# Late rows of a feed-forward, taken between later down projections instead of in the first two groups

## The chip, the cores and the metric

The kernel runs on one core of one Trainium2 chip. The metric is the time of one execution in microseconds of the device, smaller is better. The engines are TensorE (PE in the profile, its weight loads PEld), VectorE (DVE), ScalarE (ACT), GpSimd (POOL) and SyncE (SP), which issues nearly all DMAs in one queue that is worked in order. Each engine, too, takes its instructions in a fixed order.

## The reference

One layer of an encoder on 2048 rows of 1024 numbers (float32). An RMS norm, a combined projection, two kinds of attention and an output projection come first; what matters here is what follows:

```python
h = h + jnp.einsum('bse,ed->bsd', mix, w_out[l])      # output projection, residual

u2 = rms_norm(h, norm2_w[l])
gate = jnp.einsum('bsd,df->bsf', u2, w_gate[l])       # D_FF = 2816
up = jnp.einsum('bsd,df->bsf', u2, w_up[l])
h = h + jnp.einsum('bsf,fd->bsd', jax.nn.silu(gate) * up, w_down[l])
```

## The kernel before

Every matrix product is made of float16 parts: an operand is split into a high and a low half, and three products (high by high, high by low, low by high) are added up. In the feed-forward each 2 x 2 block product is formed with seven products instead of eight (Strassen's way, as Winograd arranged it), so a weight has seven combinations, each with two halves (`[P, 7, 2, 512]`), and so has an operand X.

The feed-forward works in two halves of 1024 rows, and in each half in 11 groups of 256 of the 2816 inner columns: 22 steps, half 0 first. The groups are counted from zero in the code (`fg`) and in the loop (`i`); the third group is `fg` 2. One step does `gate` (84 matrix instructions in seven products, L1030), then `up` (84 more), which multiplies the two and writes the product's combinations into an `act` tile (two buffers). After every second group comes a `down`, with two act tiles and two `wd` tiles (168 instructions, L1138): it stands at the third, fifth, seventh group and so on, between that step's gate and up. `down` takes the residual rows from DRAM (`hd`) into tiles `hs` (four buffers of 128 x 1024 float32, two in a pair), adds to them (L1144), and stores them back (L1187).

While a step computes, the weights of the next one are prepared. `load_ffn` is a generator: it fetches a weight into one of two `stages` buffers (L923, L925), squares it on ScalarE into the only `sq` buffer (L190 or L954), has TensorE find the column sums (`fsc`, L963, or L183 for a down weight), derives a scale by small VectorE operations, and writes the halves: the high ones on ScalarE (L216) or GpSimd (L220), the low ones on VectorE (L221), the combinations' sums on GpSimd (L98). The finished weight is also stored to DRAM (`split`, L919), and half 1 loads it from there (L944). Gate and up weights share two buffers (`wgu`), down weights have two of their own (`wd`). Where the generators advance is written out by hand: `quad`, which does the seven products of a gate or an up, calls a hook after each product (`at(1)` to `at(7)`), and `in_gate` and `in_up` move the generators from there. In a `quad` the second sum of products into `pd` has to wait for the evacuation of the first one (L1057 on VectorE).

The operands X are the normalised rows of `h`, transposed, combined and split. For rows 0 to 1535 that is done in the output projection (`post`). The last four tiles of 128 rows (12 to 15, the row pairs `j` = 2 and 3 of half 1) are left for later, since half 1 needs them only at step 11: these are the **late rows**. `build_x` does them, as a generator with `yield` between its pieces: load of the gain and of two row tiles (L1191, L1203), norms (`norm_tile`: a square on ScalarE, L226, the power on GpSimd, L156, the scaling on VectorE, L229), 16 transposes on TensorE (L1213, behind the last matrix instruction written so far) with ScalarE copying back (L1214), and `x_ops`: four combinations (L98) and four pieces of splitting, the high half on ScalarE (L89), the low one on VectorE or GpSimd (L98), each stored to `xcd` (L238). It takes all four `hs` buffers (as `bx`) for the gain, two row tiles and scratch, and one of the two `wd` buffers (as `b16`) to store from. The line `late_at` says after which products of which steps it moves on: those of the first two groups. Hooks 1 to 7 are those of the gate, 8 to 14 those of the up.

The order of the instructions on each engine is made by a scheduler of the programming framework from the order of the program, in which the earlier instruction has the higher priority, and from its own model of when each can start. So what stands earlier in the program usually, but not always, comes first on an engine. Which engine splits what is picked by running sums of estimated cost (`pick`, `to16`, `tt`).

Of the kernel before, what the change touches and what calls it, by code (L numbers as in the profile page):

```python
# [11 lines left out]
F32 = mybir.dt.float32  # L12
F16 = mybir.dt.float16
# [3 lines left out]
ALU = mybir.AluOpType  # L17
# [4 lines left out]
S, D, P = 2048, 1024, 128  # L22
# [37 lines left out]
def block(tc, a, out):  # L60
    nc = tc.nc
    PE, ACT, DVE, POOL, SP = nc.tensor, nc.scalar, nc.vector, nc.gpsimd, nc.sync
    top = ExitStack()
    with top:
# [44 lines left out]
        def nm(s):  # L109
            uid[0] += 1  # L110
            return f"{s}{uid[0]}"
# [57 lines left out]
        hd = dr.tile([NT, P, D], F32, name="hd")  # L169
# [87 lines left out]
        with ExitStack() as ph1:  # L257
# [24 lines left out]
            r_1, p_1, _ = norm_gain(None, w1[:, :D])  # L282
# [591 lines left out]
        with ExitStack() as ph2:  # L874
# [9 lines left out]
            fd = ph2.enter_context(tc.tile_pool(name="fd", bufs=2, reuse_waits="tile"))  # L884
# [8 lines left out]
            r_2, p_2, r_24 = rp2  # L893
            scales = {}

            rows = []
            front = [None]

            def behind():
# [5 lines left out]
            def stage(fg, nme):  # L905
                st = stages[:, turn[0]]
                turn[0] ^= 1
                f0 = 256 * fg
                with tc.issue_after(rows[1].ins) if (fg, nme) == (1, "u") else nullcontext():
                    fetch(st, f0, nme)  # L910
                store(0)
                return st

# [7 lines left out]
            def fetch(st, f0, nme):  # L921
                if nme == "d":
                    SP.dma_start(st.rearrange("p (f n) -> p f n", f=2), a["w_down"][0, f0 : f0 + 256, :].rearrange("(f p) n -> p f n", p=P))  # L923
                else:
                    SP.dma_start(st.rearrange("p (k n) -> p k n", k=KT), a["w_gate" if nme == "g" else "w_up"][0, :, f0 : f0 + 256].rearrange("(k p) n -> p k n", p=P))  # L925
# [149 lines left out]
            def gate(W, X, hooks):  # L1075
# [11 lines left out]
                note("A", 2000)  # L1087
                return sg

            def up(W, X, sg, hooks, final=False):  # L1090
                if final:
                    act = stages[:].rearrange("p b n -> p (b n)").bitcast(F16)[:, :7168].rearrange("p (o s n) -> p o s n", o=7, s=2)
                else:
                    act = fp.tile([P, 7, 2, 512], F16, tag="act", bufs=2, name=nm("act"))

                def put(o, src):
                    ACT.copy(act[:, o, 0], src)  # L1097
                    note("A", 500)
                    tt(act[:, o, 1], src, act[:, o, 0], ALU.subtract, 512, LE)

                def on_up(f, t, c):
                    s = sg[f, t][:]
                    DVE.scalar_tensor_tensor(s, c[:], W["F"][:], s, op0=ALU.mult, op1=ALU.mult)  # L1103
                    if (f, t) != (0, 1):
                        put({(0, 0): 0, (1, 0): 1, (1, 1): 3}[f, t], s)
                        return
                    a11, a12, a21, a22 = (sg[k][:] for k in ((0, 0), (1, 0), (0, 1), (1, 1)))
                    s3 = fp.tile([P, 512], F32, tag="cu", bufs=CU, name=nm("cu"))
                    tt(s3[:], a11, a21, ALU.subtract, 512, SE)
                    tt(a21, a21, a22, ALU.add, 512, SE)  # L1110
                    put(2, a21)
                    tt(a11, a21, a11, ALU.subtract, 512, SE)
                    tt(a12, a12, a11, ALU.subtract, 512, SE)
                    put(6, a12)
                    put(4, a11)
                    put(5, s3[:])

                quad(W["u"], X, "cu", CU, on_up, hooks)
                note("D", 2440)
                return act  # L1120
# [66 lines left out]
                        SP.dma_start(out[t * P : (t + 1) * P, :] if last else hd[t], hs[j][q][:])  # L1187

            def build_x():
                w2f, xa, xb, xt = (hp.tile([P, D], F32, tag="hs", bufs=4, name=nm("bx")) for _ in range(4))  # L1190
                SP.dma_start(w2f[:], a["norm2_w"].partition_broadcast(P))  # L1191
                DVE.tensor_scalar(w2f[:], w2f[:], r_24[:], None, op0=ALU.mult)
                b16 = fd.tile([P, 7, 2, 512], F16, tag="wd", bufs=2, name=nm("b16"))[:].rearrange("p o s n -> p (o s n)")
                n = [0]

                def bufs():
                    n[0] = (n[0] + 1) % 3
                    return b16[:, 2048 * n[0] : 2048 * n[0] + 2048]

                d2 = lambda z: z[:].rearrange("p (d n) -> p d n", d=2)  # L1200
                for j in (2, 3):
                    for q, z in enumerate((xa, xb)):
                        rows.append(SP.dma_start(z[:], hd[8 + 2 * j + q]))  # L1203
                    yield
                    for z in (xa, xb):
                        norm_tile(z[:], z[:], w2f[:], xt[:])
                    yield
                    for z in (xa, xb):
                        for h in range(2):
                            tr = pst("xtr")  # L1210
                            with behind():
                                for k in range(4):
                                    PE.transpose(tr[:, P * k : P * k + P], z[:, 512 * h + P * k : 512 * h + P * k + P], id32[:])  # L1213
                            ACT.copy(z[:, 512 * h : 512 * h + 512], tr[:])  # L1214
                        note("A", 1000)
                    yield
                    yield from x_ops([d2(z) for z in (xa, xb)], d2(xt), 1, j, bufs, "AP", "DP")

            W = {}
            X = [None] * 7  # L1220
# [20 lines left out]
            fp = ph2.enter_context(tc.tile_pool(name="fp", bufs=2, reuse_waits="tile"))  # L1241
# [3 lines left out]
            def tick(n):  # L1245
                for _ in range(n):
                    next(ticks, None)

            tick(1)
            load_now(0, 0, "d", W)  # L1250

            steps = [(h, f) for h in range(2) for f in range(NFG)]
            units = []
            hs = None
            chains = {}
            late_at = ((5, 9, 10, 11, 12, 13, 14), (3, 7, 8, 9, 10, 11, 12))
            for i, (half, fg) in enumerate(steps):
                if i == NFG:
                    load_x(1, XL)
                due = (len(units) == 2 and i + 1 < len(steps)) or (fg == 0 and units)  # L1260
                if due:
                    dh = steps[i - 1][0]
                    hs = [load_hs(dh, 0)]
                Wn = {}
                more = i + 1 < len(steps)

                def go(key, n=1):
                    for _ in range(n):
                        next(chains.get(key, iter(())), None)

                def start(key, *args):
                    chains[key] = load_ffn(*args)
                    go(key)

                def row(s):
                    if i < 2 and s in late_at[i]:
                        tick(1)

                def in_gate(s):
                    if s == 1:  # L1280
                        if more:
                            start("g", *steps[i + 1], "g", Wn)
                    elif s < 5:
                        go("u")
                    elif s == 5:
                        go("u", 9)
                        if more and i > 0:
                            start("d", half, fg, "d", W)
                    else:
                        go("g")  # L1290
                    row(s)

                def in_up(s):
                    if s < 3:
                        go("g")
                    elif s == 3:
                        go("g", 9)
                        go("d")
                        if more:
                            start("u", *steps[i + 1], "u", Wn)  # L1300
                    elif s < 6:
                        go("d")
                    elif s == 6:
                        go("d", 9)
                    else:
                        go("u")
                    row(7 + s)

                sg = gate(W, X, in_gate)
                if not more:  # L1310
                    load_now(half, fg, "d", W)
                if due:
                    down(dh, units, hs, dh != half, lambda: go("g"))
                    units = []
                act = up(W, X, sg, in_up, not more)
                if more and steps[i + 1][0] == 1:
                    go("u", 9)
                units.append((W, act))
                if not more:
                    down(half, units, [load_hs(half, 0, True)], True)  # L1320
                W = Wn
# [24 lines left out]
```

## Time and profile before

| | us |
|---|---|
| median of 3 runs | 2681.76 (2677.7 to 2685.48) |
| the profiled execution | 2682.59 |
| its span (first to last instruction) | 2680.8 |
| start of the feed-forward's gate in it | 1427.2 |
| mean granted TensorE clock | 0.984 of full speed |

The busy times of the engines come with their share of the span. In a row of a wait stand the engine, what it did then, the engine that ended the wait with its line, and the total, the count and the longest in us. In a row of the timeline stand the start and length in us, the engine, the line, the operation, the tiles (out<-in) with the shape, the count, and in brackets the idle time before it and what ended that. In a row of a tile's or line's instructions stand the least, median and greatest duration in ns. A busy TensorE is not TensorE at its peak, and its ends are modelled.

### The profile page before, as it was taken

To read this page: it belongs to the slowest core of one execution; us is meant where nothing else is said; L and a number is where in the kernel's file an instruction comes from. 1 tells how busy PE (TensorE), PEld (TensorE's weight loads), DVE (VectorE), ACT (ScalarE), POOL (GpSimd) and SP (SyncE) were. 2 spreads that over 40 slices of the span, in tenths; PEclk is the share of its full clock that TensorE was granted. 3 is DMA by queue.
4 is the path that set the end of the run, shared out by engine and by line. 5 is a ranking of instruction groups with operands and counts; after the bars stand their busy time and mean duration, and the time that the engine had idled before them with its cause. 6 is when DMAs were issued, how large, how long until landed. Compare 5 with 4: busy or idle time off the path is not lost. (4 is left out here: it accounts for less than half of the span.)

```text
span 2680.8 us, 50579 instructions
## 1 busy us (share of the span) xinstructions
PE 2492.4 (93%) x19628; PEld 1498.6 (56%) x19628; DVE 1932.7 (72%) x3711; ACT 1347.0 (50%) x2487; POOL 1489.1 (56%) x1098
## 2 busy tenths in 40 slices
PE   6998989888988989889989899999999999999999
PEld 4655656577776776557775344444444444444444
DVE  6898969898989989877766868777685544444434
ACT  4665656567978878665644535344352112111121
POOL 2578667667767766546764656565564232322323
PEclk9999999999999999999999899999999999999999
DMA  6777697767998979987897574665649743635532
GB/s 222 213 162 181 146 200 168 179 143 184 193 179 179 185 160 209 210 191 217 218 285 282 208 250 178 255 226 202 245 183 346 293 177 143 233 141 186 195 111 95
DMA packets 619585, 534.41 MB, mean 199 GB/s; under 512 B 480640, under 2 KB 548224, under 8 KB 609104
## 3 DMA queue, kind: packets, MB, share of 16 engines
q1 hardware_dynamic: 617520, 529.09, 69.9%
q8 instruction: 154, 2.52, 0.4%
q0 software_dynamic: 512, 1.36, 0.2%
q14 instruction: 87, 0.71, 0.1%
q10 hardware_dynamic: 1312, 0.72, 0.1%
HBM read 261.08 MB, written 147.32 MB: 152 GB/s over the span
## 5 line engine op out<-in xcount | busy, mean ns | idle before, releaser
L98 POOL TENSOR_TENSOR s<-z,s 128x1024 f16<-128x1024 f32 (+7 forms) x288 | 472.0, 1647 | 142.5 <-ACT s L89 109.8
L507 PE MATMUL sc<-kT,qT 128*128 128x512 f16 (+3 forms) x1520 | 382.0, 353 | 53.3 <-DVE z L623 19.3
L622 DVE TENSOR_TENSOR_SCAN z<-z,sc 128x512 f32<-128x512 f32 (+3 forms) x320 | 352.8, 1112 | 58.6 <-ACT sc L620 38.0
L1138 PE MATMUL pd<-wd,act 128*128 128x512 f16 x1764 | 390.9, 379 | 1.2 <-DVE cg L1071 1.2
L326 PE MATMUL pj<-w,xt 128*128 128x384 f16 x1920 | 352.2, 331 | 18.8 <-ACT xt L683 6.9
L1030 PEld LDWEIGHTS <-wg 128*128 128x128 f16 x1848 | 182.0, 99 | 230.2 <-issue 16.4
L518 PE MATMUL yp<-v,aT 128*128 128x64 f16 (+1 forms) x4896 | 269.8, 204 | 41.6 <-DMA aT<-s 40.2
L518 PEld LDWEIGHTS <-aT 128*128 128x128 f16 x4896 | 237.5, 99 | 120.4 <-DMA aT<-s 52.5
L1030 PEld LDWEIGHTS <-wu 128*128 128x128 f16 x1848 | 180.7, 98 | 218.0 <-issue 2.6
L98 POOL TENSOR_TENSOR act<-cg,act 128x512 f16<-128x512 f32 x112 | 148.5, 1337 | 262.9 <-ACT act L1097 150.8
L1138 PEld LDWEIGHTS <-act 128*128 128x128 f16 x1764 | 172.8, 98 | 209.4 <-issue 2.8
L326 PEld LDWEIGHTS <-xt 128*128 128x128 f16 x1920 | 187.3, 99 | 147.5 <-issue 21.4
L89 ACT CAST s<-z 128x128 f16<-128x128 f32 (+7 forms) x215 | 173.1, 809 | 134.1 <-DMA aT<-s 40.5
L98 POOL TENSOR_TENSOR hs<-hs,cu 128x512 f32<-128x512 f32 x99 | 130.9, 1328 | 171.3 <-DVE hs L1144 70.8
L619 ACT ACTIVATE z<-sc,c 128x512 f32<-128x512 f32 (+3 forms) x320 | 210.7, 663 | 25.6 <-PE sc L507 11.7
L1097 ACT CAST act<-cg 128x512 f16<-128x512 f32 x126 | 77.3, 616 | 238.4 <-DVE cg L1103 162.7
L507 PEld LDWEIGHTS <-qT 128*128 128x128 f16 x1520 | 128.4, 99 | 121.0 <-DVE z L623 23.0
L832 PE MATMUL po<-wo,mt 128*128 128x256 f16 x1536 | 180.7, 277 | 13.9 <-DVE xf L835 8.4
L1030 PE MATMUL pm<-X,wu 128*128 128x512 f16 x792 | 180.4, 379 | 1.3 <-DVE wu L221 1.3
L1030 PE MATMUL pm<-X,wg 128*128 128x512 f16 x792 | 181.3, 382 | 0.0
L342 PE MATMUL pj<-xt,w 128*128 128x128 f16 x2304 | 175.0, 220 | 6.7 <-DVE v L364 5.7
L1144 DVE SCALAR_TENSOR_TENSOR hs<-pd,c,hs 128x512 f32<-128x512 f32 x136 | 99.0, 747 | 109.6 <-PE pd L1138 83.1
(266 smaller groups left out, 4737.6 us busy)
## 6 DMA issues: line engine op xcount, KB each, us to landing
xt<-xs SPq DMA_DIRECT2D x112, 512.0 KB, 4.3
hs<-hd SPq DMA_DIRECT2D x68, 512.0 KB, 4.5
hd<-hs SPq DMA_DIRECT2D x56, 512.0 KB, 4.7
split<-wg SPq DMA_DIRECT2D x11, 1792.0 KB, 7.8
split<-wu SPq DMA_DIRECT2D x11, 1792.0 KB, 6.7
split<-wd SPq DMA_DIRECT2D x11, 1792.0 KB, 7.2
wg<-split SPq DMA_DIRECT2D x11, 1792.0 KB, 7.3
wd<-split SPq DMA_DIRECT2D x11, 1792.0 KB, 12.2
```

The source lines that it names most:

```text
L89: ACT.copy(dst, src)
L98: (DVE if e == "D" else POOL).tensor_tensor(dst, a_, b_, op)
L326: PE.matmul(pj[:, :384], lhsT=xv[:, xi, kt, :], rhs=G["w"][:, wi, kt, :], start=n == 0, stop=n == 23)
L342: PE.matmul(o, lhsT=x_ if c == 2 else w_, rhs=w_ if c == 2 else x_, start=n == 0, stop=n == 23)
L507: last = PE.matmul(sc[:, : 128 * w].rearrange("p (t n) -> p t n", n=P), lhsT=G["q"][i // 4][:, a_, i % 4, :], rhs=G["k"][q][:, b_, 0:w, :] ...
L518: PE.matmul(yp[:, y0 : y0 + wd], lhsT=aT[:, a_, :], rhs=v[:, v_ : v_ + wd], start=start and j == 0 and q == 0, stop=stop and j == nb - 1 a ...
L619: ACT.activation(om[:, lo:hi], sc[:, :w], AF.Sigmoid, scale=G["nkz"][:])
L622: DVE.tensor_tensor_scan(ov, ov, sc[:, :w], om[:, hi : hi + 1], op0=ALU.mult, op1=ALU.bypass)
L832: PE.matmul(po[:, sl], lhsT=mt[:, kt, P * xi : P * xi + P], rhs=wos[2 * h + n][wi][:, kt, :], start=q == 0, stop=q == 23)
L1030: front[0] = PE.matmul(ps_[:].rearrange("p (t n) -> p t n", n=P), lhsT=wv[:, wo, wi, 128 * kt : 128 * kt + 128], rhs=X[xo][:, :, xi, kt, : ...
L1138: front[0] = PE.matmul(po[:], lhsT=act[:, ao, xi, 128 * j : 128 * j + 128], rhs=W["d"][:, wo, wi, :], start=start and u == 0 and q == 0, s ...
L1144: DVE.scalar_tensor_tensor(dst, po[:], kd[:], src, op0=ALU.mult, op1=ALU.add)
```

## The change

`build_x` no longer takes its `hs` buffers once for both pairs of rows, but for each pair, with the gain loaded and scaled again each time; the row tiles are loaded ahead of the gain. Its pieces move to the up of the third group and the gate of the fourth (pair 2), and to the up of the fifth and the gate of the sixth (pair 3). It stores from the act tile that the next up will fill, which is therefore taken earlier, and no longer from a `wd` buffer. The order that put the fetch of the second group's up weights behind the second row load is gone, and so is the first piece ahead of the first down weight.

```diff
-            rows = []
...
-                with tc.issue_after(rows[1].ins) if (fg, nme) == (1, "u") else nullcontext():
-                    fetch(st, f0, nme)
+                fetch(st, f0, nme)
...
+            acts = []
+
+            def new_act():
+                return fp.tile([P, 7, 2, 512], F16, tag="act", bufs=2, name=nm("act"))
+
             def up(W, X, sg, hooks, final=False):
...
-                    act = fp.tile([P, 7, 2, 512], F16, tag="act", bufs=2, name=nm("act"))
+                    act = acts.pop() if acts else new_act()
...
             def build_x():
-                w2f, xa, xb, xt = (hp.tile([P, D], F32, tag="hs", bufs=4, name=nm("bx")) for _ in range(4))
-                SP.dma_start(w2f[:], a["norm2_w"].partition_broadcast(P))
-                DVE.tensor_scalar(w2f[:], w2f[:], r_24[:], None, op0=ALU.mult)
-                b16 = fd.tile([P, 7, 2, 512], F16, tag="wd", bufs=2, name=nm("b16"))[:].rearrange("p o s n -> p (o s n)")
                 n = [0]
 
                 def bufs():
                     n[0] = (n[0] + 1) % 3
-                    return b16[:, 2048 * n[0] : 2048 * n[0] + 2048]
+                    return acts[0][:].rearrange("p o s n -> p (o s n)")[:, 2048 * n[0] : 2048 * n[0] + 2048]
...
                 for j in (2, 3):
+                    w2f, xa, xb, xt = (hp.tile([P, D], F32, tag="hs", bufs=4, name=nm("bx")) for _ in range(4))
                     for q, z in enumerate((xa, xb)):
-                        rows.append(SP.dma_start(z[:], hd[8 + 2 * j + q]))
+                        SP.dma_start(z[:], hd[8 + 2 * j + q])
+                    SP.dma_start(w2f[:], a["norm2_w"].partition_broadcast(P))
                     yield
+                    DVE.tensor_scalar(w2f[:], w2f[:], r_24[:], None, op0=ALU.mult)
                     for z in (xa, xb):
                         norm_tile(z[:], z[:], w2f[:], xt[:])
                     yield
...
+                    acts.append(new_act())
                     yield from x_ops([d2(z) for z in (xa, xb)], d2(xt), 1, j, bufs, "AP", "DP")
+                    yield
...
-            tick(1)
             load_now(0, 0, "d", W)
...
-            late_at = ((5, 9, 10, 11, 12, 13, 14), (3, 7, 8, 9, 10, 11, 12))
+            late_at = {2: (9, 11, 13), 3: (1, 2, 3, 4, 5), 4: (9, 11, 13), 5: (1, 2, 3, 4, 5)}
...
                 def row(s):
-                    if i < 2 and s in late_at[i]:
+                    if s in late_at.get(i, ()):
                         tick(1)
```

## The prediction

> **What bounds the kernel now.** I read the page's sums first, then the busy time by windows over the first half of the feed-forward, then TensorE's waits there, then the timeline around each wait.
>
> ```profile
> span 2680.8 us, 50579 instructions
> PE 2492.4 (93%) x19628; PEld 1498.6 (56%) x19628; DVE 1932.7 (72%) x3711; ACT 1347.0 (50%) x2487; POOL 1489.1 (56%) x1098
> ```
>
> TensorE is busy 93% of the span. The feed-forward starts at about 1427 us. A window below is a stretch of the span with the busy time of each engine in it, then the mean granted clock. The first three hold groups 1 and 2 and the gate of group 3; 1582 to 1660 and 1694 to 1778 lie between two down projections.
>
> ```profile
> 1427.00:1469.00 42.00, 39.56 (x196) 19.08 (x195) 27.41 (x43) 22.90 (x28) 18.18 (x13) 1.00 0.64 234
> 1469.00:1508.00 39.00, 33.53 (x163) 16.39 (x161) 32.44 (x44) 23.14 (x33) 24.38 (x18) 0.91 0.46 162
> 1508.00:1548.00 40.00, 32.29 (x142) 14.66 (x140) 35.17 (x48) 20.08 (x25) 26.78 (x16) 0.91 0.66 228
> ...
> 1582.00:1621.00 39.00, 39.00 (x187) 18.27 (x186) 28.83 (x46) 16.23 (x21) 17.67 (x12) 1.00 0.56 187
> 1621.00:1660.00 39.00, 39.00 (x191) 18.70 (x190) 30.05 (x53) 23.42 (x28) 24.90 (x18) 1.00 0.57 220
> ...
> 1694.00:1734.00 40.00, 39.34 (x188) 18.26 (x187) 31.89 (x47) 15.70 (x20) 22.80 (x16) 1.00 0.58 204
> 1734.00:1778.00 44.00, 40.70 (x192) 19.11 (x191) 36.16 (x56) 26.65 (x32) 25.76 (x18) 0.97 0.53 201
> ```
>
> Only the first three and the last have TensorE well below the length of the window, and only those have a clock below 1. What it waited for, 1427 to 1560 first, then 1560 to 2010 (after 2010 the same view has no line):
>
> ```profile
> PE fsc L963 <- ACT sq L954: 5.9, 1, 5.9
> PE pd L1030 <- DVE cg L1057: 5.5, 1, 5.5
> PE pd L1030 <- DVE cu L1057: 2.0, 2, 1.4
> PE pd L1138 <- DVE cg L1071: 1.2, 1, 1.2
> PE pd L1030 <- DMA X<-xcd: 1.0, 1, 1.0
> ```
> ```profile
> PE pd L1030 <- DVE cg L1057: 3.5, 2, 3.3
> PE pm L1030 <- DVE wu L221: 1.3, 2, 0.7
> ```
>
> So the feed-forward bounds the time by TensorE except for 15.6 us of waits in its first 121 us and 4.8 us later. All but the DMA wait are VectorE running late (the ScalarE one too: its square waits for the weight split before it). A wait also costs clock. Twelve products take 2.75 us at full clock:
>
> ```profile
> 1491.13 4.76 PE L1030 MATMUL pd<-X,wg 128*128 128x512 f16 x12 [5.47 <-DVE cg L1057]
> ...
> 1533.90 1.87 PE L963 MATMUL fsc<-sq,ones 128*128 128x256 bf16 x8 [5.88 <-ACT sq L954]
> 1535.56 7.34 PE L1030 MATMUL pm<-X,wg 128*128 128x512 f16 x24
> ```
> ```profile
> 1773.91 4.13 PE L1030 MATMUL pd<-X,wg 128*128 128x512 f16 x12 [3.30 <-DVE cg L1057]
> ```
>
> Against 2.75 for twelve and about 5.4 for 24 these lose 2.0, 2.0 and 1.4 us; the eight of 1533.90 lose about 0.8. So the early loss is 15.6 + 4.8 = **20.4 us**, the one in 1694 to 1778 is 0.66 + 3.3 + 1.4 = 5.4.
>
> **What the change removes.** The row work itself, both row pairs together (the windows of 1427 to 1548, of the instructions on the tiles bx alone, their sum; then rows of two views of single instructions):
>
> ```profile
> sum 121.00, PE 4.20 PEld 3.63 DVE 21.73 ACT 16.00 POOL 17.59; mean PE 1.40 PEld 1.21 DVE 7.24 ACT 5.33 POOL 5.86
> ```
> ```profile
> L98 DVE TENSOR_TENSOR b<-bx,b x5: 1046/1692/2609, 1468.3 to 1513.4; 128x1024 f16<-128x1024 f32 x3, 128x512 f16<-128x512 f32 x2
> L229 DVE SCALAR_TENSOR_TENSOR bx<-bx,xrs,bx x4: 1906/2160/2284, 1448.8 to 1491.0; 128x1024 f32<-128x1024 f32 x4
> ```
> ```profile
> 1445.33 0.75 DVE L1192 TENSOR_SCALAR bx<-bx,c 128x1024 f32<-128x1024 f32 x1 [4.27 <-DMA bx<-in_norm_w_dram]
> ```
>
> With four small operations of 0.15 us on VectorE that is 22.3 us there, 16 on ScalarE, 17.6 on GpSimd (and its power operations), and 4.2 on TensorE. Out of the first 121 us VectorE's demand falls from 95.0 to 72.7 us. TensorE's own work there is 121 - 20.4 = 100.6 us, 4.2 of it the transposes that move, so VectorE's share falls from 94% to about 75%. The windows 1582 to 1660 have 58.9 of 78 us, 76%, and no wait. So nearly all of the 20.4 us goes. What is late next: the wait of 1.0 us for X stays (its load is issued ahead of the rows'), and three weight preparations in a row without a down projection between them can leave a small wait at the third gate, as at 1773.91; I keep 2 us for it. Freed: 20.4 - 1.0 - 2 = **17.4 us**. The two SP edits of that place (the up weights of group 2 no longer issued behind the second row load; the second wd buffer no longer lent to the rows) I cost at nothing: they only make loads earlier, and behind the waits above none is a DMA of a weight.
>
> **What it adds.** The same work, and one more gain load and its 0.75 us scaling, comes at two places: up of group 3 and gate of group 4, then up of group 5 and gate of group 6. Per pair that is (22.3 + 0.75) / 2 = 11.5 us on VectorE, 8 on ScalarE, 9 or more on GpSimd, 2.1 on TensorE (moved, so no sum). Three things decide what is exposed.
>
> First, when the rows can start. They take the four hs buffers that the down projection has just stored from.
>
> ```profile
> 1590.50 0.86 SPq L1187 DMA_DIRECT2D hd<-hs  x2
> ```
> ```profile
> 1704.48 0.40 SPq L1187 DMA_DIRECT2D hd<-hs  x1
> ```
> ```profile
> hs<-hd SPq DMA_DIRECT2D x68, 512.0 KB, 4.5
> hd<-hs SPq DMA_DIRECT2D x56, 512.0 KB, 4.7
> ```
>
> The last stores land about 1596 and 1709, a load takes 4.5 us more, so the norms start near 1600 and 1710. The prefetch of the next down projection's hs tiles moves behind the rows, to about 1625 and 1740; those tiles are first used after 1660 and 1778, and I cost that at nothing (if a late row holds them past that, the first accumulations slip). On SP the new stores to xcd stand in front of weight loads; the weight stage has two buffers and I count nothing, at most the 1 to 2 us by which a fetch could miss.
>
> Where the next act tile serves as the store buffer, the following up writes it only after four products, over 10 us behind the last store: nothing, unless the rows run 10 us late. The scaling of the gain is a wait that is new at both places: before it VectorE stood 4.3 us for the gain's load, and queued behind it now are the evacuations of the up products and the split of wd. Here that load is issued with the stores' end, while VectorE has gaps; 0 to 4 us, I take 0.
>
> Second, how full VectorE is after that start. Between 1598 and 1619 it waits once:
>
> ```profile
> DVE wu L221 <- ACT wu L216: 1.2, 1, 1.2
> ```
>
> Third, who waits for it. The up weights of groups 4 and 6 are written into a buffer that is free only after the previous up, and used at once:
>
> ```profile
> 1616.76 0.68 DVE L1057 TENSOR_TENSOR cg<-pd,cg 128x512 f32<-128x512 f32 x1
> ...
> 1618.68 0.59 PE L1030 MATMUL pa<-X,wu 128*128 128x512 f16 x2
> ...
> 1619.11 2.75 PE L1030 MATMUL pd<-X,wg 128*128 128x512 f16 x12
> ```
> ```profile
> 1732.51 0.68 DVE L1057 TENSOR_TENSOR cg<-pd,cg 128x512 f32<-128x512 f32 x1
> 1732.65 1.69 PE L1030 MATMUL pm<-X,wu 128*128 128x512 f16 x7 [0.66 <-DVE wu L221]
> ```
>
> In the first place L1057 ends 1.7 us before the product that needs it, so the slack is about 2 us; in the second TensorE already waits. In the program the two norms and the first x operations stand ahead of that evacuation of pd (L1057) and ahead of the weight split, so on VectorE they are queued in front of both. Of the 11.5 us I take 8 as queued there (two norms at 2.16, the scaling, 0.3 of small ones, about 3 of the splits and differences; the rest may fall to GpSimd or come later). First place: 8 less 2 of slack less 1 of idle time is a wait of 5, plus 2 of lost clock: 7. Second: 8 less the same 1 of idle time, plus 2 of clock: 9, less the 0.66 that is there already: 8.3. The gate at 1773.91 then has 3 us more of VectorE work behind it; VectorE waits for others some 7 us in that window, so I add 1. Added: 7 + 8.3 + 1 = 16.3 us.
>
> The bounds of this term: 4 + 4, if only one norm stands before the evacuation, and, by the density of the windows, more: VectorE's share would be (58.9 + 11.5) / 78 = 90% and (68.1 + 11.5) / 78.6 = 101% of TensorE's work. The windows of before lose 0 at 76%, 5.4 at 68.1 / 78.6 = 87%, and 20.4 x 78 / 100.6 = 15.8 at 94%: 1.5 us a point. That gives 10 at 90% and about 26 at 101%, so 10 + 26 - 5.4 = 31 added. I put the value between, nearer to the queue's own count: 19. **Sum:** 2682.59 - 17.4 + 19 = 2684 us. The profiled execution lies 0.8 us over the median of the runs shown, 2681.76, which is nothing here.
>
> One row bears on the price of the splits.
>
> ```profile
> L221 DVE SCALAR_TENSOR_TENSOR wu<-sq,c,wu x11: 1273/1909/1918, 1414.8 to 2008.4; 128x1024 f16<-128x1024 f32 x11
> ```
>
> The same operation takes 1.27 us or 1.9. The Trainium skill says under GPSIMD Engine Reference, section 8 (Key points), that GpSimd shares its SBUF interfaces with VectorE, so that it contends with VectorE instructions that have two inputs in SBUF. By that rule the rows' share on GpSimd also stretches the weight splits beside it, by up to 0.6 us each; with eight such splits in a window this would add some 5 us a window, and the sum would be 2694. By that rule, the trace agrees that the stretch exists; that GpSimd causes it is not shown by this row.
>
> **The rivals.** *The rows sink in* (faster): VectorE takes one norm before the evacuation and the rest while it now waits for products; each place costs 4 us, clock included. For it: the early loss came at 94% and the first place is below that. Against: the one wait of 1.2 us that VectorE has there. Time: 2682.6 - 17.4 + 4 = 2669 if the second place shows no more than the 5.4 it has, 2673 if it costs 4 too. *VectorE becomes the bound in the second place* (slower): the window 1694 to 1778 is asked for 79.6 us of VectorE beside 78.6 of TensorE, so its up weights, the L1057 evacuation and the next gate's are late one after another. It decides from the point where the demand passes TensorE's work, which the sum just reaches. Price 31: 2682.6 - 17.4 + 31 = 2696. *It doesn't do what it says*: the early waits stay, since the weight preparation itself, with one square buffer, is late; then half of the 17.4 isn't freed, and the time is 2693. Against it stands the 76% window without a wait.
>
> **How the numbers follow.** Rows about as dear as before (2676 to 2690): 0.38. Rows sink in: 0.27. VectorE the bound: 0.31; the early waits stay: 0.04. A difference of 0.3%, 8 us, is about what a measurement of this kernel can tell. So faster 0.27, same 0.38, slower 0.35. The range takes in 2669 and most of 2696's side: 2668 to 2700; left out are a gain of nearly the whole 17.4 (under 0.1) and waits that pile up further (0.1).
>
> **What would show it.** Right: no wait over 2 us before 1540 and clock 1.00 in the windows there; the first down projection starts some 18 us earlier; one TensorE wait of 4 to 7 us on L1057 or wu L221 at the end of the gates of groups 4 and 6, with a clock under 1 each. Wrong on the faster side: those gates run without waits. Wrong on the slower side: waits on wu or L1057 also at the gate of group 7, or TensorE's transposes (L1213) waiting for the norms.

## The result and the profile after

The changed kernel takes 2692.31 us (median of 8 runs, 2689.81 to 2697.79), the kernel before 2683.33 us in 8 runs beside it: a ratio of 1.0041, 95% interval 1.0029 to 1.0052. It is 9 us slower. The profiled execution took 2693.41 us, with a span of 2691.6. Its sums hardly differ from those of before, so the difference isn't work:

```profile
span 2691.6 us, 50594 instructions
...
PE 2494.5 (93%) x19628; PEld 1498.8 (56%) x19628; DVE 1934.3 (72%) x3711; ACT 1345.5 (50%) x2488; POOL 1484.3 (55%) x1098
```

To place it I cut the feed-forward in each trace at the 13th matmul of each down projection. Segment 1 holds the groups 1 and 2 and the gate of group 3 (the old place of the rows), segment 2 the first new place, segment 3 the second. The feed-forward is the span less the start of its first gate, which differs among the profiled executions (1419.9 to 1431.7); segments that an edit leaves alone agree within 1.5 us. All kernels of the study, one profiled execution each, in us:

| kernel | 1 | 2 | 3 | 4 | 5 | rest | feed-forward |
|---|---|---|---|---|---|---|---|
| before | 123.0 | 111.8 | 119.6 | 112.2 | 111.0 | 676.0 | 1253.6 |
| after | 101.8 | 131.7 | 134.6 | 111.8 | 111.0 | 676.0 | 1266.9 |
| e1_no_rows | 101.8 | 111.8 | 118.1 | 112.2 | 111.0 | 675.9 | 1230.8 |
| e2_row_seven | 102.3 | 129.8 | 120.6 | 131.0 | 111.0 | 675.9 | 1270.7 |
| e3_act_in | 102.1 | 127.1 | 136.3 | 111.8 | 111.0 | 676.0 | 1264.2 |
| e4_late_norm | 101.8 | 131.2 | 133.8 | 111.8 | 111.0 | 675.9 | 1265.7 |
| e6_norm_behind | 101.8 | 121.6 | 139.7 | 111.8 | 111.0 | 676.1 | 1262.1 |
| e7_dve_only | 101.8 | 123.5 | 133.4 | 112.2 | 111.0 | 675.9 | 1257.7 |
| e8_act_queue | 102.5 | 122.5 | 133.3 | 111.8 | 111.0 | 676.5 | 1257.6 |
| e9_norm_only | 101.8 | 120.8 | 126.7 | 112.2 | 111.0 | 676.0 | 1248.5 |
| e10_split_pairs | 113.8 | 121.0 | 119.5 | 111.8 | 111.0 | 676.0 | 1253.1 |
| e11_spread | 113.5 | 121.3 | 119.6 | 111.8 | 111.0 | 676.0 | 1253.3 |
| e12_rows_after_x | 114.1 | 120.8 | 118.7 | 112.2 | 111.0 | 676.0 | 1252.7 |
| e13_norm_behind2 | 113.6 | 122.9 | 118.1 | 112.2 | 111.0 | 676.9 | 1254.6 |

After against before: segment 1 gives 21.2 back, segment 2 takes 19.9, segment 3 takes 15.0, and nothing else moves. The windows of after say the same. The first two lie in segment 1 (compare the clock of 0.91 that this place had before), the next two in the first new place, the last two in the second. The columns are length, PE, PEld, DVE, ACT and POOL with their counts, the granted clock, the DMA share and GB/s:

```profile
1458.00:1490.00 32.00, 32.00 (x158) 15.32 (x157) 24.12 (x37) 17.48 (x22) 18.05 (x14) 1.00 0.33 130
1490.00:1524.00 34.00, 30.72 (x147) 14.32 (x146) 29.18 (x42) 18.80 (x23) 23.11 (x16) 1.00 0.52 189
1558.00:1612.00 54.00, 43.36 (x204) 20.41 (x202) 35.92 (x52) 22.44 (x32) 26.29 (x17) 0.94 0.57 183
1612.00:1655.00 43.00, 40.07 (x187) 18.73 (x186) 32.95 (x56) 24.17 (x30) 24.05 (x18) 0.96 0.55 206
1690.00:1744.00 54.00, 44.42 (x207) 20.90 (x206) 43.99 (x58) 23.40 (x33) 29.68 (x20) 0.92 0.60 214
1744.00:1789.00 45.00, 41.70 (x189) 19.09 (x187) 35.65 (x55) 26.04 (x32) 27.00 (x19) 0.92 0.55 207
```

TensorE's waits of after from 1540 to 2010, where before had 4.8 us after 1560:

```profile
PE pd L1028 <- DVE cg L1055: 10.2, 2, 6.9
PE pd L1028 <- DVE c L205: 6.4, 1, 6.4
PE xtr L1215 <- DVE bx L229: 4.7, 4, 2.7
PE fsc L961 <- ACT sq L952: 3.8, 2, 2.9
PE pm L1028 <- DVE cu L1069: 1.3, 1, 1.3
PE pm L1028 <- DVE wu L221: 0.7, 1, 0.7
```

One of the six is new in kind: the transposes of the rows (L1215) wait for their norms. The wait of 6.4 us is put down to L205, one of the small operations that make a weight's scale, but it is the wait on the evacuation of `pd` again (L1055, the L1057 of before). The product starts at 1608.10, 0.05 us behind the end of that evacuation, as the one with the 6.9 us starts 0.06 us behind its own in the second place. VectorE's timeline of after:

```profile
1607.37 0.68 DVE L1055 TENSOR_TENSOR cg<-pd,cg 128x512 f32<-128x512 f32 x1
1607.96 0.14 DVE L205 TENSOR_SCALAR c<-c 128x1 f32<-128x1 f32 x1
```

The products behind these waits are slow as before the change, TensorE's timeline of after:

```profile
1608.10 4.73 PE L1028 MATMUL pd<-X,wg 128*128 128x512 f16 x12 [6.40 <-DVE c L205]
...
1618.35 1.31 PE L961 MATMUL fsc<-sq,ones 128*128 128x256 bf16 x8 [2.93 <-ACT sq L952]
1619.45 6.80 PE L1028 MATMUL pm<-X,wu 128*128 128x512 f16 x24
```

So the first place adds up: 6.4 + 3.8 + 3.4 (the longest transposes' wait of 2.7 and one of 0.7) are 13.6 us of waits; the lost clock is 4.73 - 2.75 = 2.0, about 0.3, and 6.80 less 5.3 for 24 products; with the 2.1 us of the transposes themselves it is 19.5 of the 19.9 measured.

Why VectorE is late there is seen one step further back. SyncE's queue of after, with the stores of the down projection (L1190) and the loads of the rows (L1203) and of the gain (L1204):

```profile
1555.87 0.32 SPq L1190 DMA_DIRECT2D hd<-hs  x1
1560.72 0.32 SPq L1203 DMA_DIRECT2D bx<-hd  x1
1561.13 0.38 SPq L1190 DMA_DIRECT2D hd<-hs  x1
1566.40 0.32 SPq L1203 DMA_DIRECT2D bx<-hd  x1
1566.82 0.86 SPq L1190 DMA_DIRECT2D hd<-hs  x2
1572.12 0.33 SPq L1204 DMA_DIRECT2D bx<-in_norm_w_dram  x1
```

Each load goes out some 5 us after the store ahead of it, that is, when the store has landed and the buffer is free; the next store stands behind the waiting load in the same queue. VectorE meets the rows so:

```profile
1574.73 0.15 DVE L155 TENSOR_SCALAR xrs<-xss 128x1 f32<-128x1 f32 x1 [8.38 <-ACT bx L226]
1576.14 0.75 DVE L1206 TENSOR_SCALAR bx<-bx,c 128x1024 f32<-128x1024 f32 x1 [1.26 <-DMA bx<-in_norm_w_dram]
1576.81 0.68 DVE L1050 TENSOR_TENSOR cu<-pm,cu 128x512 f32<-128x512 f32 x1
```

It stands 8.4 us in front of an operation of 0.15 us, with the evacuations of the up (L1050 is one) behind it, in the stretch where it could have worked ahead. From this come two theories of the price.

**Late data**: the stores, the loads behind them and VectorE's order make it idle, and what it misses there is missing later. Then other buffers, another queue or a later place for the norms give most of the price back. **Too much work**: VectorE is full enough between two down projections that 11.5 us more of it are paid whenever they are done, and the idle 8.4 us would have been lost or not. A third is the density of the prediction: the price grows with VectorE's share of the place, so a less filled place is cheap.

### The profile page after: what moved, and what is told of

The parts are those of the page before. It is cut to its first block, busy times and chain, and to the rows that moved or that the text cites. A ratio compares the mean times of both kernels' runs of the same rounds, so it can differ in the third digit from the quotient of the medians.

```text
span 2691.6 us, 50594 instructions
## 1 busy us (share of the span) xinstructions
PE 2494.5 (93%) x19628; PEld 1498.8 (56%) x19628; DVE 1934.3 (72%) x3711; ACT 1345.5 (50%) x2488; POOL 1484.3 (55%) x1098
## 4 chain that ended last, share of the span: by engine, by line
PE 42%; DVE 10%; issue 4%; DMA 3%; POOL 3%; ACT 2%; SPq 0%; DVEq 0%; ACTq 0%; POOLq 0%
PE pd L1141 12%; PE pm L1028 10%; PE pd L1028 7%; PE pa L1028 7%; DVE z L622 2%; PE po L832 2%; DMA hd<-hs 1%; DVE wd L221 1%; POOL s L98 1%; DMA aT<-s 1%; DVE cg L98 1%; DVE z L623 1%; PE pj L326 1%; DVE wu L221 1%; DVE wg L221 1%
## 5 line engine op out<-in xcount | busy, mean ns | idle before, releaser
L326 PE MATMUL pj<-w,xt 128*128 128x384 f16 x1920 | 353.3, 332 | 18.1 <-ACT xt L683 7.7
```

The costliest lines, as they stand in the source:

```text
L326: PE.matmul(pj[:, :384], lhsT=xv[:, xi, kt, :], rhs=G["w"][:, wi, kt, :], start=n == 0, stop=n == 23)
```

## The experiments

Those that leave work out say so in their expectation. The kernel before ran beside each of them, and the ratio is to those runs.

**e1_no_rows**: the price of all late rows.

```diff
-late_at = {2: (9, 11, 13), 3: (1, 2, 3, 4, 5), 4: (9, 11, 13), 5: (1, 2, 3, 4, 5)}
+late_at = {}
```

> Leaves out the four late row tiles: their operands are not made, and half 1 takes those of its first two row pairs twice. Both theories expect the early waits gone as in the changed kernel and no new ones between the down projections, so this prices the rows: the stretch from the start of the feed-forward to its first down projection about 99.6 us as in the changed kernel (120.8 before), the two stretches after it about 111.5 and 118 as before, the time about 21 us under before, 2662. If early waits come from the weight preparation itself, more is left and it is nearer 2670.

2661.11 us, ratio 0.9925 (0.9902 to 0.9948). Segment 1 has the 101.8 us of after to the tenth. So the change takes away as much of the early loss as leaving the rows out does (both keep 3.6 us of waits at the first down projection), and 1266.9 - 1230.8 = 36.1 us is the price of the rows in the new places, against 1253.6 - 1230.8 = 22.8 in the old. Both hold the 4.2 us of the transposes.

**e2_row_seven**: pair 3 from the steps 4 and 5 to 6 and 7, a less filled place.

```diff
-..., 4: (9, 11, 13), 5: (1, 2, 3, 4, 5)}
+..., 6: (9, 11, 13), 7: (1, 2, 3, 4, 5)}
```

> Pair 3 in the up of the seventh and the gate of the eighth group, where VectorE has as much room as at the first place (58.0 of 77 us busy before). Late data (the row tiles' buffers have to be stored from first, store and load one behind the other in SP's queue, and VectorE and TensorE wait for them in order): the schedule there is that of the first place, so pair 3 costs 20 us as pair 2 does instead of 15, about 2697. Too much VectorE work between two down projections: at 90% instead of 101% of TensorE's work pair 3 costs less, 10 instead of 15, about 2687.

2698.25 us, ratio 1.0061 (1.0041 to 1.0082). Segment 4 goes from 112.2 to 131.0, 18.8 us, as much as the first place, while segment 3 keeps 120.6. A place without a wait of its own is no cheaper than the one that I had counted at 101%, so density doesn't tell the price. (The loads are as late here as in the first place, so this says nothing of the price of the work alone.) TensorE's waits there, from 1778 to 1925, are those of the first place:

```profile
PE pd L1028 <- DVE c L175: 6.1, 1, 6.1
PE fsc L961 <- ACT sq L952: 3.5, 2, 2.7
PE xtr L1215 <- DVE bx L229: 2.9, 2, 2.2
```

**e3_act_in**: rows into the next act tile, so that they wait for no store of the down projection.

```diff
+acts.append(new_act())
+av = acts[0][:].rearrange("p o s n -> p (o s n)").bitcast(F32)
+xa, xb, xt = (av[:, D * k : D * k + D] for k in range(3))
-w2f, xa, xb, xt = (hp.tile([P, D], F32, tag="hs", ...) for _ in range(4))
+w2f, *hb = (hp.tile([P, D], F32, tag="hs", ...) for _ in range(4))
```

> The roles of the buffers swapped: the row tiles and the scratch are taken from the next act tile, free as soon as the down projection's last matrix instruction has read it, and the gain and the three store buffers are the hs tiles. Late data: no row load waits for a store of the down projection, VectorE's 8.4 us wait and TensorE's 3.4 us at the transposes at the first place go, that place costs 8 to 10 instead of 20, the second some 3 less than its 15: about 2678. Too much VectorE work: the same operations at the same hooks, at most 2 us better, 2690.

2690.07 us, 1.003 (1.0016 to 1.0044), the first place 4.6 us cheaper than in after, the second 1.7 dearer. It didn't take the lateness away, so it doesn't tell the theories apart: the loads moved behind the stores in the same queue, and the buffer of the gain still waited for a store. SyncE's queue, then VectorE's waits from 1555 to 1625:

```profile
1560.21 0.33 SPq L1207 DMA_DIRECT2D bx<-in_norm_w_dram  x1
1560.63 7.17 SPq L1190 DMA_DIRECT2D hd<-hs  x2
1567.85 1.25 SPq L1206 DMA_DIRECT2D act<-hd  x2
```
```profile
DVE xrs L155 <- ACT act L226: 7.0, 1, 7.0
DVE bx L1209 <- DMA bx<-in_norm_w_dram: 5.5, 1, 5.5
```

**e4_late_norm**: the norms' piece two slots later in the program.

```diff
-late_at = {2: (9, 11, 13), ..., 4: (9, 11, 13), ...}
+late_at = {2: (9, 13, 14), ..., 4: (9, 13, 14), ...}
```

> The same pieces, but norms after the sixth and transposes after the seventh product of the up instead of the fourth and sixth. Late data: the norms stand behind more of the up's evacuations, VectorE no longer waits 8.4 us for them, the first place costs some 6 us less, about 2686. Too much VectorE work: nothing is taken away and the rows come nearer to the up weights that are used at once, 2692 to 2696.

2692.92 us, 1.0043 (1.0027 to 1.006). The scheduler put the first small operation as early as before, and VectorE stood 7.2 us in front of it. Nothing follows for either theory, except that the place in the program alone doesn't set the place on the engine.

**e6_norm_behind**: the norms held on VectorE behind the up's accumulation of its sixth product, the x operations two slots later.

```diff
+evac[0] = DVE.tensor_tensor(u3[:], u3[:], p4[:], ALU.subtract).ins
...
+with tc.issue_after(evac[0]):
     DVE.tensor_scalar(w2f[:], w2f[:], r_24[:], None, op0=ALU.mult)
     for z in (xa, xb):
         norm_tile(z[:], z[:], w2f[:], xt[:])
```

> The norms' VectorE operations are queued behind the evacuation after the up's sixth product (they follow that hook, 13), the transposes and what follows come at gate hooks 2 to 7. Late data: VectorE has done the up's evacuations before it meets a row that isn't there, its wait of 8.4 us and TensorE's at the transposes go, the first place costs 8 to 10 instead of 20, about 2681. Too much VectorE work: the row operations now stand right in front of the splits of the up weights, nothing is saved, 2692 to 2697.

2691.14 us, 1.0033 (1.0018 to 1.0048). VectorE no longer stands for the square in the first place, which falls from 131.7 to 121.6; the second rises from 134.6 to 139.7. TensorE's waits in the first place are now 5.7 us in four; in the second 17.7, L1056 (L1055 of after) in front. The same edit takes late data out of one place and makes the other dearer. That it does so by pushing work into the next gate is my reading of the wait on L1056, and not shown by a run of its own.

**e7_dve_only**: the rows out, and VectorE alone given as much work in the same slots.

```diff
-    for z in (xa, xb):
-        norm_tile(...)
+    DVE.memset(acts[0][:, 0], 0.0)
+    work(8)   # adds of 128 x 512 f32
...
-    yield from x_ops(...)
+    for _ in range(4):
+        work(2)
+        yield
```

> Leaves out the late rows (half 1 takes the operands of its first two row pairs twice) and puts in their places VectorE operations alone, on an otherwise unused piece of the next act tile: eight of 0.7 us at the hook of the norms, two at each of four hooks of the gate, some 11.5 us a pair with a clearing, without a load to wait for, a transpose, or work on another engine. Against the kernel without rows, 2661: too much VectorE work expects most of the price in the same stretches, 10 at the first place and 12 at the second, about 2683. Late data expects 5 or less at the first place and 8 at the second, about 2673.

2686.25 us, 1.0005 (0.9996 to 1.0015); 25 us over no rows by the medians, 27 by the feed-forwards of the table. The two segments of e1_no_rows, then of this kernel (VectorE is the third busy time):

```profile
1526.00:1638.50 112.50, 112.50 (x540) 52.88 (x539) 83.95 (x130) 49.97 (x61) 67.49 (x47) 1.00 0.60 216
1638.50:1756.70 118.20, 114.07 (x550) 53.81 (x549) 89.44 (x136) 56.22 (x65) 70.66 (x49) 1.00 0.63 234
```
```profile
1529.50:1653.00 123.50, 116.37 (x535) 53.11 (x533) 93.05 (x146) 49.21 (x60) 65.13 (x47) 0.96 0.54 193
1653.00:1786.30 133.30, 119.47 (x549) 55.03 (x548) 100.51 (x154) 56.62 (x66) 68.96 (x49) 0.95 0.57 207
```

VectorE was busy 9.1 and 11.1 us longer than without rows; in after it is 10.7 and 11.8. There is no load, no wait for a load and no transpose here, and the places still cost 11.7 and 15.3 us. So work alone gives 15.3 of the 16.5 us of the second place (over no rows), and 11.7 of the 19.9 of the first. TensorE's waits from 1530 to 1790, all but one on VectorE:

```profile
PE pd L1028 <- DVE cg L1055: 10.4, 2, 7.1
PE pd L1028 <- DVE c L175: 4.5, 1, 4.5
PE pm L1028 <- DVE wu L221: 3.4, 1, 3.4
PE pa L1028 <- DVE wu L221: 1.9, 1, 1.9
PE pa L1028 <- ACT cu L1041: 0.7, 1, 0.7
```

VectorE isn't full there: from 1550 to 1630 it stands 22.7 us for residual rows and for products of TensorE. What makes its work dear is that it stands in front of what TensorE waits for: an added operation of 1.69 us is the last one ahead of the evacuation that ends the 4.5 us. (It is put down to L175, the operation behind that evacuation.) An order on VectorE in which the added work always yields to the evacuations was not tried.

**e8_act_queue**: e3 with its loads on ScalarE's queue, where no store stands.

```diff
-SP.dma_start(z, hd[8 + 2 * j + q])
+ACT.dma_start(z, hd[8 + 2 * j + q])
...
-SP.dma_start(w2f[:], a["norm2_w"].partition_broadcast(P))
+ACT.dma_start(w2f[:], a["norm2_w"].partition_broadcast(P))
```

> As the run that read the rows into the act tile, but the gain's and the rows' loads issued from ScalarE's queue, where nothing stands before them but a copy, and not from SP's behind the stores of the down projection. Late data: the rows land some 5 us after the last matrix instruction of the down projection, VectorE's wait for the first norm falls from 7 to 2 us or less, the first place costs about 12 instead of the 15 of that run, the time is about 2684. Too much VectorE work: the same as that run, 2690.

2686.97 us, 1.0009 (0.9997 to 1.0021). The first place is at 122.5, 9.2 less than in after; the second at 133.3, 1.3 less. VectorE now stands 1.0 us for the square, and before that 6.7 us for the gain, with two accumulations of the down projection next behind it, and TensorE doesn't wait there. TensorE has one wait in the first place, from 1555 to 1635, for the evacuation that the row work stands in front of:

```profile
PE pd L1028 <- DVE cg L1055: 6.5, 1, 6.5
```

So late data is 9.2 us of the first place and 1.3 of the second. The waits say the same of the first: of those of after, the transposes' 3.4 us are gone, and the square's 3.8 with the 1.8 of clock behind it, 9.0 together; the evacuation's 6.4 stays, as 6.5. What is left, 10.7 and 15.2 over no rows, is what e7 gave for work (11.7 and 15.3), though e7 has no transposes. Two ways that share no edit agree to about 3 us.

**e9_norm_only**: the x operations left out, loads, norms and transposes kept.

```diff
-yield from x_ops([d2(z) for z in (xa, xb)], d2(xt), 1, j, bufs, "AP", "DP")
+for _ in range(5):
+    yield
```

> Keeps the rows' loads, norms and transposes at their hooks and leaves out the combinations, splits and stores (half 1 takes the operands of its first two row pairs twice): about half of the rows' VectorE work is gone, all waits for data stay. Late data: the first place still costs 13 to 15 of its 20, the second 6. Too much VectorE work: the first place costs 8 or less, the second 5. By late data 2680, by too much work 2672.

2676.99 us, 0.9972 (0.9959 to 0.9985), between the two expectations. The places cost 9.0 and 8.6 us. VectorE is busy 3.3 and 4.6 us longer than without rows, so more than half of the added work is gone, with the same late loads as in after and the same idle 8.4 us. The largest of TensorE's waits from 1530 to 1850 is that of the transposes:

```profile
PE xtr L1215 <- DVE bx L229: 6.2, 3, 3.1
```

The waits of 6.4 and 6.9 us on L1055 have shrunk to 0.2 or nothing (the 3.3 at the gate of group 7 is in before too). So the x operations were what that evacuation queued behind, and the late norms are the larger part of what is left. The two terms don't simply add.

Then whether a version beats both kernels. Pair 2 goes back to the first group, pair 3 stays in the first new place with the loads of e8.

**e10_split_pairs** and **e11_spread**:

```diff
+for j in (2, 3):
+    if j == 2:   # hs tiles, stored from the second wd buffer, as before
...
+    else:        # as e8
...
-late_at = {2: ..., 3: ..., 4: ..., 5: ...}
+late_at = {0: (5, 8, 9, 10, 11, 12, 13), 2: (9, 11, 13), 3: (1, 2, 3, 4, 5)}             # e10
+late_at = {0: (5, 8, 9, 11, 13), 1: (2, 4), 2: (9, 11, 13), 3: (1, 2, 3, 4, 5)}          # e11
```

> Pair 2 is built in the first group, as in the kernel before (loads ahead of the feed-forward, all its work in the first gate and the first up), pair 3 in the third group's up and the fourth gate with its rows in the next activations' tile and its loads on ScalarE's queue. The first 120 us of the feed-forward have 101.8 us with no rows at all and 123.0 with both pairs; the place of pair 3 cost 10.7 us with these loads. If a pair costs about the same 10 to 12 us wherever it is put (VectorE has no room anywhere), the early pair costs 10 to 11 us and the time is 2681 to 2683. If what counts is the idle time that VectorE has there (it is busy 54 and 62% of the first 35 us without rows, which leaves 14 us for the pair's 11.5), the early pair costs 3 to 5 us, the first segment is 105 to 107, and the time is 2675 to 2677, faster than both kernels.

> As the kernel that splits the pairs, but pair 2 spread from the first gate to the second (ticks at 5, 8, 9, 11, 13 and at 2 and 4 of the second gate, where VectorE is 86% busy without rows). Same price wherever it is put: the same 2681 to 2683. By idle time: 1 to 4 us worse than the dense one, since part of the work falls into the fuller second gate, 2677 to 2680.

2680.44 us, 0.9995 (0.9983 to 1.0006), and 2678.85 us, 0.9989 (0.9976 to 1.0002): no different from before. The early pair costs 12.0 and 11.7 us, where I had hoped for 3 to 5 from VectorE's idle time in the first 35 us. In e11 the first norm starts 24 us into the feed-forward (1443.7) and the x operations at 1458.2, when those 35 us are over. The pair is paid like any other. The guess from idle time, my own, fell a second time.

**e12_rows_after_x** and **e13_norm_behind2**: the last of the late data out of both places.

```diff
+silu[0] = ACT.activation(s[:], c[:], AF.Silu, scale=W["kg"][:]).ins
...
+with tc.issue_after(silu[0]) if j == 2 else nullcontext():
     for q, z in enumerate((xa, xb)):
         ACT.dma_start(z, hd[8 + 2 * j + q])
     ACT.dma_start(w2f, a["norm2_w"].partition_broadcast(P))
     yield
+with tc.issue_after(last[0]) if j == 2 else nullcontext():             # e12
+with tc.issue_after(last[0] if j == 2 else evac[0]):                   # e13
     DVE.tensor_scalar(w2f, w2f, r_24[:], None, op0=ALU.mult)
```

> As the spread kernel, but the rows of the early pair are loaded from ScalarE's queue behind the first gate's first activation, so behind the last X load, and its norms stand on VectorE behind the first gate's last accumulation, so that none of that gate's work queues behind them. In the spread kernel the early segment was 113.5 us: 11.7 over no rows, with TensorE waiting 3.0 us for X, 2.4 for a weight on ScalarE and 6 us in four smaller waits, while VectorE stood 7.4 us for the norm's square. If late data is half of a pair's price, the wait for X and the one on ScalarE go, the early segment is 107 to 109 and the time 2672 to 2675. If the price is VectorE's and ScalarE's work alone, the segment stays at 112 to 114 and the time at 2678 to 2680.

> As the kernel with the rows behind X, and the late pair's norms too stand behind the second up's accumulation of its third product, its x operations one tick later each. In the kernels so far that place cost 9.5 us over no rows with the loads on ScalarE's queue (121.3 against 111.8) and 9.8 with the norms put back but the loads on SP's queue. If each removes its own part of late data, the place is at 117 to 119 and the time 2 to 4 us under the kernel with the rows behind X. If what is left is work, the place stays at 121 to 122 and the two kernels are equal.

2675.96 us, 0.9993 (0.9983 to 1.0003), and 2681.01 us, 1.0011 (0.9999 to 1.0023). VectorE no longer stands for the rows in the first gate, and the early pair still costs 12.3 and 11.8 us; pair 3 costs 9.0 and 11.1. TensorE's waits of e12 from 1420 to 1535:

```profile
PE pd L1029 <- DMA X<-xcd: 3.2, 1, 3.2
PE pm L1029 <- DVE wu L221: 2.0, 1, 2.0
PE pd L1142 <- ACT cg L1082: 1.9, 1, 1.9
PE pm L1029 <- ACT wu L216: 1.8, 1, 1.8
PE pd L1142 <- DVE cg L1070: 1.6, 1, 1.6
```

The wait for X stayed although the rows now load behind it. The traces tell most of its cause. X's last load is issued 7.6 us after the first gate starts in every one, and lands at 16.6 us in before, 17.7 in e1 without any rows, 18.1 in after and 18.8 here. In SyncE's queue the up weights of group 2 stand ahead of it in the last three, and in before behind it and the rows. In e1 and after TensorE takes a product of the up first, and so doesn't wait. Against e1 the rows delay it by 1.1 us, about a third of the wait. For the rest the cost went from one engine's operation to the next, as the work theory expects, and no version here beats the kernel before by what can be measured.

## Why the prediction was right in its range and wrong in a step

The forecast was 2684, no change within 0.3%; the result is 0.41% slower, inside the range. It lies there by the room that the range left for the rival at 2696, and not by the sum: what is freed was right, but what is added was put at 19 us and measured 30.7.

*What bounds the kernel, and what is freed*: right in sum. The waits before 1540 are gone but for 3.6 us at the first down projection (2.0 on ScalarE, 1.6 on VectorE), the clock is 1.00 there, and the first down projection starts 21.2 us earlier into the feed-forward. Of these 4.2 are the transposes that move along, so waits and clock gave 17.0 where the sum has 17.4. That the remainder fits is luck: the sum kept 3 us for X and the third gate, where no wait came, and the 3.6 us stand elsewhere. Nor do the two SP edits *only make loads earlier*: X's last load lands 1.5 us later.

*When the rows can start*: right. The norms were put near 1600 on the timeline of before; the first down projection now lies 23.7 us earlier (1526.5 against 1550.2), and they start at 1574.7.

*What is added*: here it failed. The step said 7 us for the first place, 8.3 + 1 for the second, and chose 19 between these and 31. Measured without the transposes, it is 19.9 - 2.1 = 17.8 and 15.0 - 2.1 = 12.9, together 30.7.

- *The wait on L1057*: right. It is there at the end of both gates, 6.4 and 6.9 us with 2.0 and 2.5 of lost clock, where 5 and 7 with 2 each were forecast. In e8, where the rows' loads have another queue, it is the only wait of the first place.
- *"0 to 4 us, I take 0"* for the new wait on VectorE: this is the term that failed. The one that counts isn't the gain's (1.3 us) but the small operation after the square, 8.4 us, and I hadn't listed it as a wait at all: I had the start of the norms, and stopped there instead of asking what VectorE does until then with an instruction of theirs at the head of its queue. With the order of stores and loads on SyncE this is worth 9.2 us in the first place (e8, where the transposes' wait and the late square are gone), most of the 10.8 by which that place was short. I had named transposes that wait for norms as a sign of being wrong on the slower side, and put no price on it.
- In the second place VectorE stands only 2.3 us for the square. The 3.6 us by which this place was short are 1.4 of transposes that wait for norms, 1.3 of a wait for another evacuation (L1069), neither of which the step had, and 0.9 of lost clock.
- *The second place as the dearer one*: wrong for the whole price, 15.0 against 19.9, as the late data falls mostly on the first. For the work alone the order was right: 15.3 against 11.7 in e7, 15.2 against 10.7 in e8. The slope of 1.5 us a point was too steep for that.

The upper bound of the step, 31, was the right sum for a wrong reason: it came from the slope of density, which gives 10 for a place that cost 17.8. So the rival that VectorE becomes the bound, 2696, has the feed-forward right (2682.6 - 17.0 + 30.7 = 2696; the execution's feed-forward began 2.5 us earlier, and it took 2693.4), but not its mechanism, which needed the second place to be the costly one. *The rows sink in* is refuted by both places; *it doesn't do what it says* by segment 1.

The price of the splits: the rule of the Trainium skill on shared SBUF interfaces (GPSIMD Engine Reference, section 8, Key points) would have given 2694, near the result, by longer splits. They didn't get longer in sum: VectorE was busy 231.4 us on L221 over the span, and 232.7 before; in the segment of the first place it is 2.0 us more, in that of the second 1.3 less. So the near hit is chance. The rule itself shows in the norms, below.

## What to carry to other kernels

Work that is moved off the stretch that it delays has to be paid where it lands: before counting a gain, put as much dummy work of the same engine at the new place (e7), since the mean share of an engine over a window didn't tell the price of the places here. For a moved load, follow its data to the first instruction that waits for it and ask what that engine's queue holds behind it; a load into a buffer that is just being stored, in the queue of the stores, makes a chain of store, load, store. In e8 and e10 to e13 a pair still cost 9 to 15 us wherever it was put. Whether an order in which the rows always yield to the evacuations is cheaper, or only less of the work is, stays open.

## What the runs showed that was not expected

The norm's operation (L229, 128 x 1024 f32) takes 1.28 us in the new places and took 2.13 before, in the mean of four. VectorE's timeline of after, then of before:

```profile
1577.47 1.27 DVE L229 SCALAR_TENSOR_TENSOR bx<-bx,xrs,bx 128x1024 f32<-128x1024 f32 x1
1579.20 1.28 DVE L229 SCALAR_TENSOR_TENSOR bx<-bx,xrs,bx 128x1024 f32<-128x1024 f32 x1 [0.45 <-POOL xrs L156]
```
```profile
1448.82 2.28 DVE L229 SCALAR_TENSOR_TENSOR bx<-bx,xrs,bx 128x1024 f32<-128x1024 f32 x1
```

What GpSimd does meanwhile, of after and of before:

```profile
1577.64 1.53 POOL L156 TENSOR_TENSOR xrs<-xrs,mh 128x1 f32<-128x1 f32 x1 [2.12 <-DVE xrs L155]
```
```profile
1448.76 1.27 POOL L98 TENSOR_TENSOR sq<-stages 128x512 f32<-128x512 f32 x1
1450.11 2.12 POOL L98 TENSOR_TENSOR sq<-stages,sq 128x512 f32<-128x512 f32 x1
```

Beside GpSimd's 512 elements the operation is stretched to 2.28 us; beside its power of one element a partition it isn't. The weight splits (L221) agree: from 1420 to 2010 in before, the 35 of 1024 elements with GpSimd idle all take 1.27 to 1.29 us, the 15 with GpSimd busy for 90% of their time or more 1.78 in the mean, 1.27 to 2.28. By the rule of the Trainium skill cited above (GPSIMD Engine Reference, section 8, Key points: GpSimd contends on shared SBUF interfaces with VectorE instructions of two SBUF inputs) the trace agrees: here the stretched operations have a GpSimd operation beside them, though no run took that one away by itself. The new places made 3.4 us less VectorE work of the same four norms, and were still the dearer ones.
